# A hybrid Fourier, attention and mixture-of-experts network on one Trainium2 core: the depthwise convolution as plain float32 matmuls, the routing tables in groups of eight, splits queued behind a flag, and pools that release tile by tile

## The chip, the cores and the metric

The kernel runs on one core of one Trainium2 chip. The core has a matrix engine (TensorE, PE in the profile, with its weight loads as PEld), a vector engine (VectorE, DVE), a scalar engine (ScalarE, ACT), GpSimd (POOL) and SyncE (SP), which here only issues DMA transfers. Each engine works through its own queue in order. The metric is the device time of one execution in microseconds; less is better.

## What is computed

Two layers over 2048 tokens of 1024 channels, with a small context. Layer 0 mixes tokens by a Fourier transform of half of its channels and a windowed attention of the rest; layer 1 is a convolution module; behind each stands a mixture of 16 experts, of which each token takes two. All of it is float32.

```python
def _conformer_conv(h, pw1_w, pw1_b, dw_w, dw_b, ln_g, ln_b, pw2_w, pw2_b):
    a, g = jnp.split(h @ pw1_w + pw1_b, 2, axis=-1)
    u = a * jax.nn.sigmoid(g)
    u = lax.conv_general_dilated(u, dw_w[:, None, :], ...,      # 31 taps, each channel by itself
                                 feature_group_count=u.shape[-1]) + dw_b
    u = jax.nn.silu(_layernorm(u, ln_g, ln_b))
    return u @ pw2_w + pw2_b

def _grouped_moe(h, router_w, router_b, w_gate, w_up, w_down):
    scores = jax.nn.sigmoid(t @ router_w)
    ...                                   # best group of 4 by its top two, then the top 2 experts in it
    order = jnp.argsort(flat_e)           # the assignments sorted by expert,
    padded = (counts + 127) // 128 * 128  # each expert's in blocks of 128 slots
    ...
    def expert_block(args):
        tok, e = args
        xb = t_pad[tok]
        return (silu(xb @ w_gate[e]) * (xb @ w_up[e])) @ w_down[e]
```

## The kernel before

**Products.** Nearly every product of two float32 matrices is made of three matmuls of a shorter float type (written fp32r): a number is split into a high part `h` (a cast, by ScalarE) and a low part `l` (the number less its high part, by VectorE, in some places GpSimd), and `mm3` (lines 76 to 82) adds hh, hl and lh. `split` (line 70) issues the cast and the subtraction.

**Stages.** In order: attention (0 to some 640 us), the Fourier part (fold, transform, output; to 900), the routing of the first experts (900 to some 1005), 41 blocks of the first experts (to 1880), the convolution's first matrix pw1 (to 2282), the depthwise convolution (to 2496), pw2 with layer norm (to 2800), the second routing and the second experts.

**The convolution** (`_conv`, lines 1497 to 1552). The 1024 channels are 64 groups of 16, and a tile has 16 channels by 8 phases of the tokens on its 128 partitions and 256 positions along them (token = 8 x position + phase). A group's convolution is five matmuls with banded 128x128 weights, each for the same data shifted by one position; the bands `th`, `tl` are the tap table `wth`, `wtl` times a mask `mk` that keeps each channel to itself. The loop runs over 32 steps of two groups: fetch `u` from memory (SP), split it twice, once for each of two shifts (`uh`, `ul`: ScalarE and VectorE), for each group make `th` (VectorE) and `tl` (GpSimd), run five times `mm3` (15 matmuls of 256 columns), add the bias while emptying PSUM (ScalarE, line 1539) and store `v` (ScalarE's queue). In the first eight steps the weights of pw2 are loaded and split too, and behind every fourth step SP loads `v` back for what follows.

**The routing** (`tail_start`, `choose`, `route`, `moe`). For each tile of 128 tokens the router's logits are made (`lgs`, `lgp`), the experts ranked on VectorE (`E`, one-hot rows), and counted by matmuls (`pr`). For the last two tiles, 14 and 15, the normalised row is made by `last()` at the end of the tail, by a copy on ScalarE and two operations on GpSimd (line 914). Then `route` builds a table of 6144 slots (`tab`, 32 matmuls over `vt`, line 1122): `vt` holds for each slot column n and tile t whether the token of this row belongs there, laid out [n, t], and each matmul picks one t out of every 16 elements. `slot_i` is the list of tokens by slot; `gather` (GpSimd, an indirect DMA, line 1187) fetches the tokens of a block into `xg`, and `xtr` transposes and splits them. The weights of the first block come as six tiles `raw` and are split by `wsplit` into `wh` (ScalarE) and `wl` (four operations for a tile): tile 0 on GpSimd behind the last normalisation, the other five on VectorE behind `placed`, the making of `slot_i`.

**The order** comes from a scheduler that places instructions in program order by engine, with `issue_after` holding an instruction back behind another. Buffers come from pools (`tile_pool`). A pool that opens where an older one closed takes its memory, and in this version its first users wait for all that was under way on the old pool as a whole, whichever tile they touch.

**The fold** (`_fold`, line 674) opens such pools behind the attention: `pe<-z` clears eight PSUM banks, then for each of eight channel groups VectorE builds sums and differences of `h` (`p`, `eo`, `d`, `de`, lines 697 to 707), which PE multiplies by tables (`wqh`, `wql`). The first `h` is in memory on chip already, the others are loaded by SP (line 694), and GpSimd's queue loads the tables `ch`, `cl`, `sh`, `sl`.

## Time and profile before

| | us |
|---|---|
| median of three runs | 3701.32 (3699.11 to 3705.8) |
| the profiled execution | 3704.51, its span 3702.6 |
| PE busy | 3225.4 (87%) |
| VectorE busy | 2490.0 (67%) |
| ScalarE busy | 1520.0 (41%) |
| GpSimd busy | 1003.4 (27%) |
| mean granted clock of TensorE | 0.928 |

Busy time is the time in which an engine had an instruction running. [...] The 1.9 us between span and time lie around the program. A row's number in brackets is the idle time of its engine just before it, and what ended it.

### The profile page before, as it was taken

Reading aid. Unit: us, or ns where it says so; the run is one execution under the profiler, and the core shown is the slowest. Engines: PE = TensorE matmul, PEld = TensorE weight load, DVE = VectorE, ACT = ScalarE, POOL = GpSimd, SP = SyncE. Lnnn points to the kernel's source line nnn. Section 1 sums busy time; section 2 is a strip of 40 time slices with the busy share of each in tenths; the row PEclk is TensorE's granted clock in tenths of the full one; section 3 lists DMA queues with packets and bytes.
Section 4 is the critical chain, followed back from the end, with each engine's and each line's share of the span. In section 5 each row is a group of like instructions: output and inputs, shape, how many; then the busy total and the mean of one; then the engine's idle time right before and its main releaser. Section 6 shows DMA issues by size and latency. Waiting matters only on the chain. (4 is left out here: it accounts for less than half of the span.)

```text
span 3702.6 us, 57945 instructions
## 1 busy us (share of the span) xinstructions
PE 3225.4 (87%) x20868; PEld 2863.5 (77%) x20868; DVE 2490.0 (67%) x5261; ACT 1520.0 (41%) x3353; POOL 1003.4 (27%) x774
## 2 busy tenths in 40 slices
PE   7899998688599899989979998776877999999997
PEld 4677776576488888888879998665666888889897
DVE  5889988758766554656463323988997687784554
ACT  4666767233344222444342222333333465561331
POOL 2343433533311111111130001554542222212221
PEclk9999999799789999999989999887987999999999
DMA  6322222454575655656532213322325676773452
GB/s 231 93 86 79 93 71 96 148 167 179 205 248 193 204 176 165 218 183 201 180 103 46 46 35 85 117 90 96 108 97 207 226 294 252 285 296 116 169 180 105
DMA packets 258094, 571.07 MB, mean 154 GB/s; under 512 B 94809, under 2 KB 142945, under 8 KB 230113
## 3 DMA queue, kind: packets, MB, share of 16 engines
q1 hardware_dynamic: 178704, 386.75, 30.0%
q0 software_dynamic: 42512, 138.39, 12.7%
q10 hardware_dynamic: 36416, 40.09, 3.2%
q8 instruction: 253, 4.15, 0.4%
q14 instruction: 209, 1.70, 0.1%
HBM read 436.12 MB, written 133.73 MB: 154 GB/s over the span
## 5 line engine op out<-in xcount | busy, mean ns | idle before, releaser
L1181 ACT CAST wh<-raw 128x512 fp32r<-128x512 f32 x768 | 455.3, 621 | 153.7 <-DVE y L1287 70.1
L1184 DVE TENSOR_TENSOR wl<-raw,wh 128x512 fp32r<-128x512 f32 x760 | 484.2, 684 | 23.5 <-ACT wh L1181 19.5
L79 PE MATMUL gps<-wh,xt0h 128*128 128x256 f32 x1344 | 403.5, 300 | 64.2 <-issue 22.8
L81 PE MATMUL gps<-wh,xt0l 128*128 128x256 f32 x1344 | 396.8, 295 | 16.0 <-DVE wl L1184 11.1
L80 PE MATMUL gps<-wl,xt0h 128*128 128x256 f32 x1344 | 395.7, 294 | 0.0
L79 PE MATMUL gps<-wh,xt1h 128*128 128x256 f32 x1280 | 368.2, 288 | 18.6 <-issue 18.6
L81 PE MATMUL gps<-wh,xt1l 128*128 128x256 f32 x1280 | 364.0, 284 | 6.5 <-DVE wl L1184 5.9
L80 PE MATMUL gps<-wl,xt1h 128*128 128x256 f32 x1280 | 363.9, 284 | 0.0
L79 PEld LDWEIGHTS gps<-wh,xt0h 128*128 128x128 f32 x1344 | 273.5, 204 | 75.6 <-issue 61.9
L1219 ACT ACTIVATE sg<-gps 128x256 f32<-128x256 f32 x164 | 63.3, 386 | 588.2 <-PE gps L81 558.0
L79 PE MATMUL ag<-hh,p1h 128*128 128x256 f32 x1024 | 292.0, 285 | 3.6 <-DVE u L1481 2.1
L1221 DVE TENSOR_TENSOR hid<-sg,gps 128x256 f32<-128x256 f32 x164 | 68.6, 418 | 333.4 <-PE gps L81 333.4
L80 PE MATMUL ag<-hl,p1h 128*128 128x256 f32 x1024 | 290.8, 284 | 0.0
L81 PE MATMUL ag<-hh,p1l 128*128 128x256 f32 x1024 | 290.6, 284 | 0.0
L1187 POOL DMA_INDIRECT xg<-f_d,slot_i x88 | 98.0, 1113 | 705.0 <-PE xps L1194 676.5
L81 PEld LDWEIGHTS gps<-wh,xt0l 128*128 128x128 f32 x1344 | 273.4, 203 | 18.5 <-DVE wl L1184 12.8
L79 PE MATMUL yps<-wh,hh 128*128 128x512 f32 x656 | 280.0, 427 | 0.0
L80 PEld LDWEIGHTS gps<-wl,xt0h 128*128 128x128 f32 x1344 | 274.1, 204 | 0.6
L79 PEld LDWEIGHTS gps<-wh,xt1h 128*128 128x128 f32 x1280 | 246.6, 193 | 22.4 <-issue 20.9
L81 PE MATMUL yps<-wh,hl 128*128 128x512 f32 x656 | 259.0, 395 | 0.0
L80 PE MATMUL yps<-wl,hh 128*128 128x512 f32 x656 | 258.4, 394 | 0.0
L81 PEld LDWEIGHTS gps<-wh,xt1l 128*128 128x128 f32 x1280 | 246.6, 193 | 6.6 <-DVE wl L1184 6.5
(846 smaller groups left out, 9099.2 us busy)
## 6 DMA issues: line engine op xcount, KB each, us to landing
raw<-in_wall SPq DMA_DIRECT2D x202, 1024.0 KB, 8.6
oh<-in_ada_w SPq DMA_DIRECT2D x24, 1024.0 KB, 8.9
racw<-in_ada_w SPq DMA_DIRECT2D x64, 256.0 KB, 2.7
x_d<-x SPq DMA_DIRECT2D x32, 512.0 KB, 6.2
f_d<-f ACTq DMA_DIRECT2D x28, 512.0 KB, 3.2
adaw<-in_ada_w SPq DMA_DIRECT2D x32, 256.0 KB, 5.5
x<-in_x SPq DMA_DIRECT2D x16, 512.0 KB, 4.2
ht_d<-hf ACTq DMA_DIRECT2D x16, 512.0 KB
```

The costliest lines, as they stand in the source:

```text
L79: mm(ps, ah, bh, start=first, stop=False)
L80: mm(ps, ah, bl, start=False, stop=False)
L81: mm(ps, al, bh, start=False, stop=last)
L1181: nc.scalar.copy(h, r)
L1184: (nc.gpsimd if pool else nc.vector).tensor_tensor(l, r, f32(h), ALU.subtract)
L1187: return self.nc.gpsimd.indirect_dma_start(self.xg[s % 2], None, self.f[self.lay], bass.IndirectOffsetOnAxis(self.slot_i[:, s:s + 1], 0))
L1219: one = nc.scalar.activation(sg, g, AF.Silu)
L1221: return one, nc.vector.tensor_tensor(hid[:, b * 256:b * 256 + 256], sg, u, ALU.mult)
```

## The change

Five things at once.

1. **The convolution** takes plain float32 matmuls on `u` itself: five for a group in place of 15, no splits of `u` or of the taps. `u` lies in six buffers with zero borders, so that a shift is an offset, and is fetched five steps ahead. `th` and the PSUM tile have four buffers each, the staging tile of pw2's weights two.
2. **Eights.** The slot table's columns are laid out [m, t, j] with n = 8m + j: each matmul reads eight adjacent elements, and the vectors that are compared and multiplied along t are made in eight copies first (`slb`, `tk8`, `tl8`, `part`).
3. **Flags.** `went` is set by GpSimd behind the second gather, VectorE copies it (`routed2`), and all six tiles' splits, now all on VectorE, are queued behind this copy. Loads of the next weights all go through SP.
4. **The last normalisation** of tiles 14 and 15 is two operations on VectorE, and tile 14's comes earlier in the program.
5. **All pools** are opened with `reuse_waits="tile"`: the first user of a new tile waits only for what used that piece of memory.

```diff
-    def wsplit(self, i, pool=False, after=None):
+    def wsplit(self, i, after=None):
...
-            (nc.gpsimd if pool else nc.vector).tensor_tensor(l, r, f32(h), ALU.subtract)
+            nc.vector.tensor_tensor(l, r, f32(h), ALU.subtract)
...
             def last():
-                with self.tc.issue_after((self.scored if i == 15 else self.copied).ins):
-                    nc.scalar.activation(f, x, AF.Copy, scale=r)
-                for op, z in ((ALU.mult, G2), (ALU.add, S2)):
-                    self.normed = nc.gpsimd.tensor_tensor(f, f, z, op)
+                nc.vector.scalar_tensor_tensor(f, x, r, G2, ALU.mult, ALU.mult)
+                nc.vector.tensor_tensor(f, f, S2, ALU.add)
...
-                eq = ys[0][:, h * i:h * i + h].bitcast(BF16).rearrange("p (n t) -> p n t", n=NS)
+                eq = ys[0][:, h * i:h * i + h].bitcast(BF16).rearrange("p (m x) -> p m x", m=M)
...
-                nc.tensor.matmul(tab, self.oh[:, i, k], vt[:, :, :, k], start=False, stop=i + k == T)
+                nc.tensor.matmul(tab, self.oh[:, i, k], vt[:, :, :, 8 * k:8 * k + 8], start=False, stop=i + k == T)
...
+                with tc.issue_after(g.ins):
+                    nc.gpsimd.memset(self.went, 1.0)
+                with tc.issue_after(self.placed.ins):
+                    went = nc.vector.tensor_copy(self.routed2, self.went)
                 for i in range(6):
-                    if i < (1,1)[lay]:
-                        with tc.issue_after(self.scored.ins), tc.issue_after(self.normed.ins):
-                            self.wsplit(i, True)
-                        with tc.issue_after(g.ins):
-                            self.load(i, 17 * lay + 1, nc.gpsimd)
-                    else:
-                        with tc.issue_after(g.ins), tc.issue_after(self.placed.ins):
-                            self.wsplit(i)
-                        self.load(i, 17 * lay + 1)
+                    with tc.issue_after(self.scored.ins), tc.issue_after(went.ins):
+                        self.wsplit(i)
+                    self.load(i, 17 * lay + 1)
...
-        UO = [[[wp.tile([P, 2, 260], F32R, name=f"u{x}{sh}{i}") for x in "hl"] for sh in range(2)] for i in range(2)]
+        U = [(up if i < 3 else wp).tile([P, 2, 260], F32, name=f"u{i}") for i in range(6)]
...
+        for b in range(5):
+            fetch(b)
         for b in range(32):
-            if b % 4 == 1 and b < 28:
-                taps(2 * b + 6)
-            u = up.tile([P, 2, 256], F32, name="u", tag="u", bufs=3)
-            nc.sync.dma_start(u, u4[:, 2 * b:2 * b + 2, :])
-            uo = UO[b % 2]
-            for sh in range(2):
-                uh, ul = uo[sh]
-                self.split(uh[:, :, 2 - sh:258 - sh], ul[:, :, 2 - sh:258 - sh], u)
+            if b < 27:
+                fetch(b + 5)
+            u = U[b % 6]
...
-                th = tp.tile([P, 5, 16, 8], F32R, name="th", tag="th")
-                tl = tp.tile([P, 5, 16, 8], F32R, name="tl", tag="tl")
-                nc.vector.tensor_tensor(th, f32(wth[:, g])[:, :, None, :].to_broadcast([P, 5, 16, 8]), mks, ALU.mult)
-                nc.gpsimd.tensor_tensor(tl, f32(wtl[:, g])[:, :, None, :].to_broadcast([P, 5, 16, 8]), mks, ALU.mult)
-                ps = pp.tile([P, 256], F32, name="cv", tag="cv")
+                th = tp.tile([P, 5, 16, 8], F32, name="th", tag="th", bufs=4)
+                nc.vector.tensor_tensor(th, wt[:, g][:, :, None, :].to_broadcast([P, 5, 16, 8]), mks, ALU.mult)
+                ps = pp.tile([P, 256], F32, name="cv", tag="cv", bufs=4)
                 for j in range(5):
-                    uh, ul = uo[j % 2]
-                    s = slice(j - j % 2, j - j % 2 + 256)
-                    a = [x[:, j].rearrange("p c q -> p (c q)") for x in (th, tl)]
-                    self.mm3(ps, a[0], a[1], uh[:, i, s], ul[:, i, s], j == 0, j == 4)
+                    nc.tensor.matmul(ps, th[:, j].rearrange("p c q -> p (c q)"), u[:, i, j:j + 256], start=j == 0, stop=j == 4)
...
-            with tc.tile_pool(name="fc", bufs=1) as cp, tc.tile_pool(name="fp", bufs=1, space=PSUM) as pp:
+            with tc.tile_pool(name="fc", bufs=1, reuse_waits="tile") as cp, tc.tile_pool(name="fp", bufs=1, space=PSUM, reuse_waits="tile") as pp:
```

VectorE's queue at the start of the convolution (`u<-ag` is the end of pw1, `ul`, `wtl` and `p2l` are low halves), before:

```order
L1481 SCALAR_TENSOR_TENSOR u<-ag,p1b,sg 128x32x8 x11
L1565 MEMSET on 128x128
L74 TENSOR_TENSOR wtl<-wt,wth 128x320
L1531 TENSOR_TENSOR th<-wth,mk 128x640
L74 TENSOR_TENSOR ul_34360<-u,uh_34359 128x2x256
L74 TENSOR_TENSOR ul_34362<-u,uh_34361 128x2x256
L1531 TENSOR_TENSOR th<-wth,mk 128x640
L74 TENSOR_TENSOR wtl<-wt,wth 128x320
```

and after:

```order
L1487 SCALAR_TENSOR_TENSOR u<-ag,p1b,sg 128x32x8 x11
L1529 TENSOR_TENSOR th<-wt,mk 128x640 x4
L1559 MEMSET on 128x128
L1529 TENSOR_TENSOR th<-wt,mk 128x640
L74 TENSOR_TENSOR p2l<-raw_34401,p2h 128x1024
L1529 TENSOR_TENSOR th<-wt,mk 128x640
```

Four bands now stand right behind pw1's last `u`, with no split between them.

VectorE's queue where the slots of the first experts are known (`routed` is the flag, `wl` a weight split, `xt0l` the first block's tokens), before:

```order
L1125 TENSOR_REDUCE slot_i<-tab 128x48
...
L1137 TENSOR_SCALAR ch<-ch 128x1
L1184 TENSOR_TENSOR wl_10073<-raw_10083,wh_10072 128x512 x4
L1184 TENSOR_TENSOR wl_10067<-raw_10084,wh_10066 128x512 x3
L74 TENSOR_TENSOR xt0l<-xps,xt0h 128x512 x2
L1184 TENSOR_TENSOR wl_10067<-raw_10084,wh_10066 128x512
L1184 TENSOR_TENSOR wl_10069<-raw_10085,wh_10068 128x512 x4
L1184 TENSOR_TENSOR wl_10075<-raw_10086,wh_10074 128x512 x4
```

and after:

```order
L1132 TENSOR_REDUCE slot_i<-tab 128x48
...
L1144 TENSOR_SCALAR ch<-ch 128x1
L1346 COPY routed<-routed 128x1
L1191 TENSOR_TENSOR wl_10069<-raw_10080,wh_10068 128x512 x3
L74 TENSOR_TENSOR xt0l<-xps,xt0h 128x512 x2
L1191 TENSOR_TENSOR wl_10069<-raw_10080,wh_10068 128x512
L1191 TENSOR_TENSOR wl_10071<-raw_10081,wh_10070 128x512 x4
L1191 TENSOR_TENSOR wl_10065<-raw_10082,wh_10064 128x512 x4
```

The copy of the flag stands ahead of the first split, three splits instead of seven stand ahead of the tokens, and 21 instead of 13 behind them before the next other work.

VectorE's queue at the logits of tile 15 (`ch<-lgs` are the logits, the operations behind them rank the experts), before:

```order
L103 TENSOR_SCALAR roots<-tny 128x1
L946 SCALAR_TENSOR_TENSOR ch<-lgs,roots,shift 128x16
L1017 TENSOR_TENSOR ch<-ch,rb 128x32
L1009 TENSOR_TENSOR ch<-ch 128x128
L1011 TENSOR_TENSOR ch<-ch,rc 128x128
```

and after:

```order
L946 SCALAR_TENSOR_TENSOR ch<-lgs,roots,shift 128x16
L911 SCALAR_TENSOR_TENSOR f<-x,roots,G_8583 128x1024
L1016 TENSOR_TENSOR ch<-ch,rb 128x32
L912 TENSOR_TENSOR f<-f,S_8588 128x1024
L1008 TENSOR_TENSOR ch<-ch 128x128
```

The two operations of the last normalisation now stand among the ranking's.

## Rows read from the trace of the kernel before

**Rows 1.** Windows: stretch, its length, each engine's busy time (instructions), granted clock, DMA.

```profile
960.00:1060.00 100.00, 68.34 (x475) 62.36 (x476) 59.70 (x136) 25.31 (x47) 27.95 (x17) 0.71 0.51 169
...
1900.00:2290.00 390.00, 380.65 (x3172) 379.98 (x3170) 132.02 (x313) 98.04 (x205) 20.19 (x30) 0.99 0.24 52
2290.00:2500.00 210.00, 152.08 (x961) 144.50 (x961) 183.83 (x162) 70.75 (x138) 121.86 (x63) 0.83 0.38 114
```

**Rows 2.** The tiles `th` and `cv`: durations (min/median/max ns), then PE's idle time (us, times) until.

```profile
L1531 DVE TENSOR_TENSOR th<-wth,mk x64: 808/825/2191, 2287.1 to 2489.2; 128x640 fp32r<-128x640 f32 x64
...
  DVE th L1531: 50.0, 19
```

**Rows 3.** Timeline, one step of the convolution: start, us, what, [idle before <- releaser].

```profile
2415.86 2.88 DVE L1531 TENSOR_TENSOR th<-wth,mk 128x640 fp32r<-128x640 f32 x2
...
2418.15 0.36 PE L79 MATMUL cv<-uh,th 128*128 128x256 f32 x1 [2.84 <-DVE th L1531]
```

**Rows 4.** Timeline, from pw1 into the convolution, and its last matmul.

```profile
2281.89 0.28 PE L81 MATMUL ag<-hh,p1l 128*128 128x256 f32 x1
...
2282.71 0.65 DVE L1481 SCALAR_TENSOR_TENSOR u<-ag,p1b,sg 128x256 f32<-128x256 f32 x1 [5.06 <-ACT sg L1479]
...
2286.23 0.46 ACT L73 CAST wth<-wt 128x320 fp32r<-128x320 f32 x1 [3.56 <-DMA u_d<-u]
...
2288.16 0.55 PE L79 MATMUL cv<-uh,th 128*128 128x256 f32 x1 [5.99 <-ACT wth L73]
...
2495.58 0.28 PE L81 MATMUL cv<-uh,tl 128*128 128x256 f32 x1
```

**Rows 5.** Float32 matmuls of other stages: tile views (ns), then timelines.

```profile
L1587 PE MATMUL mean<-sq,on x12: 378/379/382, 2550.2 to 2741.2; 128*128 128x256 f32 x12
...
L196 PE MATMUL ada<-adaw,cc x64: 592/592/1057, 6.0 to 38.1; 128*2 128x512 f32 x64
...
2549.94 0.40 PE L81 MATMUL wo<-p2h,zl 128*128 128x512 f32 x1
...
2550.17 0.59 PE L1587 MATMUL mean<-sq,on 128*128 128x256 f32 x2
...
2550.84 0.40 PE L80 MATMUL wo<-p2l,zh 128*128 128x512 f32 x1
...
2551.07 0.40 PE L81 MATMUL wo<-p2h,zl 128*128 128x512 f32 x1
...
2809.13 1.94 PE L944 MATMUL lgs<-rw,f 128*128 128x16 f32 x16
```

**Rows 6.** Timeline, the start of the Fourier fold.

```profile
679.20 1.23 DVE L697 TENSOR_TENSOR p<-h 128x1023 f32<-128x1023 f32 x1 [11.18 <-DMA x_d<-x]
...
683.94 0.56 PE L79 MATMUL pe<-wqh,eh 128*128 128x260 f32 x1 [13.73 <-ACT eh L73]
...
686.80 2.90 DVE L697 TENSOR_TENSOR p<-h 128x1023 f32<-128x1023 f32 x1 [2.77 <-DMA h<-ht_d]
```

**Rows 7.** Timeline, routing of the first experts.

```profile
964.19 2.40 DVE L96 SCALAR_TENSOR_TENSOR tna<-tny,tnv 128x1 f32<-128x1 f32 x1
...
969.51 0.22 DVE L96 SCALAR_TENSOR_TENSOR tna<-tny,tnv 128x1 f32<-128x1 f32 x1
...
980.38 0.20 PE L1034 MATMUL pr<-E,trb 128*128 128x48 bf16 x1 [14.12 <-DVE E L1027]
...
986.48 5.77 PE L1122 MATMUL tab<-xg,oh 128*128 128x96 bf16 x32 [4.34 <-DVE xg L1120]
...
993.12 4.29 DVE L1184 TENSOR_TENSOR wl<-raw,wh 128x512 fp32r<-128x512 f32 x7
...
993.38 4.94 POOL L1187 DMA_INDIRECT xg<-f_d,slot_i  x1 [11.88 <-DVE ch L1137]
```

**Rows 8.** Timeline, routing of the second experts.

```profile
2828.31 0.20 PE L1034 MATMUL pr<-E,trb 128*128 128x48 bf16 x1 [11.88 <-DVE E L1027]
...
2842.95 1.00 POOL L1187 DMA_INDIRECT xg<-f_d,slot_i  x1 [11.06 <-DVE ch L1135]
```

More of the change, by code (lines that the diff above doesn't have):

```diff
@@ L140, in route_consts @@
         nc, io = self.nc, self.io
-        cm = self.tc.tile_pool(name="rt", bufs=1, side="right")
+        cm = self.tc.tile_pool(name="rt", bufs=1, side="right", reuse_waits="tile")
         pool = cm.__enter__()
@@ L167, in route_consts @@
         self.tl = pool.tile([P, 2, NT], BF16, name="tl")
-        self.routed = pool.tile([P, 1], F32, name="routed")
+        flags = pool.tile([P, 3], F32, name="routed")
+        self.routed, self.went, self.routed2 = [flags[:, i:i + 1] for i in range(3)]
         self.E = {T: pool.tile([P, 16 * T + 16], BF16, name=f"E{T}") for T in (4, 2)}
@@ L568, in _attention @@
         self.hp.__exit__(None, None, None)
-        self.hp = self.tc.tile_pool(name="h0", bufs=1, side="right")
+        self.hp = self.tc.tile_pool(name="h0", bufs=1, side="right", reuse_waits="tile")
         self.h0 = self.hp.__enter__().tile([P, L], F32, name="h0")
@@ L641, in fourier @@
                 for nms in ("emo", "p"):
-                    yps.append(tc.tile_pool(name="fy" + nms, bufs=1, side="right"))
+                    yps.append(tc.tile_pool(name="fy" + nms, bufs=1, side="right", reuse_waits="tile"))
                     y = yps[-1].__enter__()
@@ L660, in raw_open @@
     def raw_open(self, lay, a=0, b=6):
-        cm = self.tc.tile_pool(name=f"raw{lay}{a}", bufs=1, side="right")
+        cm = self.tc.tile_pool(name=f"raw{lay}{a}", bufs=1, side="right", reuse_waits="tile")
         rp = cm.__enter__()
@@ L1445, in weights @@
                     for name, side in (("c1b", "left"), ("c1r", "right")):
-                        more.append(self.tc.tile_pool(name=name, bufs=1, side=side))
+                        more.append(self.tc.tile_pool(name=name, bufs=1, side=side, reuse_waits="tile"))
                         more.append(more[-1].__enter__())
@@ L1488, in conv_start @@
         nc, io = self.nc, self.io
-        self.cvp = self.tc.tile_pool(name="cv0", bufs=1, side="right")
+        self.cvp = self.tc.tile_pool(name="cv0", bufs=1, side="right", reuse_waits="tile")
         p = self.cvp.__enter__()
@@ L1499, in _conv @@
         up, wt, mk, db = self.cv
-        wth = wp.tile([P, 64, 5, 8], F32R, name="wth")
-        wtl = wp.tile([P, 64, 5, 8], F32R, name="wtl")
-        def taps(g):
-            s = slice(g, g + 8)
-            self.split(wth[:, s], wtl[:, s], wt[:, s])
-        taps(0)
         wh, wl = self.pw2
```

87 lines of the change are left out of this document (47 added, 40 removed).

## The prediction

> **What bounds the kernel now.** I read the table of windows first, with the stages as its stretches, to see where TensorE (PE) does not fill its time, because the dense stages are already full. The stage before the convolution keeps PE busy for 380.65 of 390 us at a clock of 0.99; the convolution has 152.08 of 210 us at 0.83; and the 100 us in which the first mixture of experts is routed have 68.34 at 0.71 [rows 1]. Those are the two kinds of place that the change rewrites.
>
> Then I read the convolution by its tile, for what PE waits for. It sits idle 50.0 us, in 19 pieces, until VectorE (DVE) has made a band of taps `th` [rows 2]. One such piece shows why: two bands take 2.88 us on DVE where an undisturbed one takes 0.825 (the median), and PE starts 2.84 us late [rows 2, 3]. DVE also makes the low halves of `u` and shares the time with GpSimd, which makes `tl`. So the convolution is fed by DVE, not held by its matmuls: pw1 runs 3172 matmuls of the same 256 columns in 380.65 us, 0.12 us each [rows 1], so the 960 of the convolution would take 115 us if fed, and the stage takes 213.7 (from the last matmul of pw1, 2281.89 + 0.28, to the last of the convolution, 2495.58 + 0.28) [rows 4].
>
> Last I read the timelines at the joints of the stages: the start of the Fourier fold, where PE is idle 13.73 us [rows 6], and the two routings, where it is idle 14.12 and 11.88 us in one piece and more behind it [rows 7, 8].
>
> **Convolution, the main term.** Removed: 640 of 960 matmuls, all work of ScalarE on `u` (two casts a step), two DVE subtractions a step, every `tl` on GpSimd, the taps' split. Added: 320 matmuls in plain float32. What one costs is the number on which this forecast rests. The trace has such a matmul, `mean<-sq,on`, 256 columns: each call shows as two records of 379 ns, side by side as "x2" in the timeline [rows 5]. Around one pair the timeline goes from 2549.94 to 2550.84 with one wo matmul, the pair and another wo matmul; wo matmuls start 0.23 apart (2550.84 to 2551.07), so the pair costs 0.90 - 2 x 0.23 = 0.44 us, 0.22 a record [rows 5]. A second way gives nearly the same: a 512-column float32 record lasts 592 ns and a 256-column one 379, so 256 columns cost 0.213 us [rows 5]. Loading 128x128 float32 weights for every record doesn't add to it: 16 float32 matmul records, each with another set of weights and 16 columns, take 1.94 us, 0.12 each [rows 5], less than 0.22. So PE needs 320 x 0.44 = 140.8 us, against 115 for the three-term product: by PE alone the change is a loss, and it gains only by what feeds it.
>
> [...]
>
> What feeds it now: per step of two groups PE needs 4.40 us. DVE has two `th` of 0.825, 1.65 us; even at the 2.88 that a disturbed pair took it would keep up [rows 2, 3]. In the first eight steps a split of 1024 elements comes on top, some 1.3 us by the 640 of a band. ScalarE keeps two evictions. GpSimd is idle, so DVE is undisturbed. `u` comes five steps (22 us) ahead in six buffers. The start: the last `u` of pw1 is written at 2282.71 + 0.65; DVE then makes the first band, 0.82, so PE starts near 2284.3 where it started at 2288.16 [rows 4], because the cast ahead of it, 3.56 us behind the store of `u` [rows 4], is gone, and the tile-wise pools carry no such wait over to `th`. From 2282.2: 2.1 + 140.8 = 143, and 1.7 for slow records behind the pause, 144.7 against 213.7. **Term: -69 us.** [...] What follows the convolution (the last store, its load, the variance, then pw2) keeps its chain, and moves with it.
>
> **The fold's start.** PE waits 13.73 us until 683.94. The chain behind it: DVE's `p<-h` starts at 679.20 after 11.18 us for the landing of the store `x_d` [rows 6]; that store has nothing to do with `h`, it is a wait that the whole pool carried. With waits by tile, `p` could start near 668 and PE 11 us sooner. But its second half, `h` of the next channel group, lands at 686.8 today (DVE waits 2.77 for it) [rows 6], and if it is asked for earlier it shares the queues with 4 MB of tables; half of the gain then comes back as a wait. Term -6, ends 0 and -11. The other joints have no such wait on their chain: 0.
>
> **Routing of the first experts.** Before, GpSimd's normalisation of the last two tiles and its four weight splits run beside DVE's small operations, and seven of these take 1 to 2.4 us (one of them takes 2.40 at 964.19 and 0.22 at its next turn, undisturbed) [rows 7]; together some 11 us, all on the chain to `E`. The change takes that work off GpSimd and puts four operations of 1024 elements on DVE, 1.23 each by the one of 1023 [rows 6]: -11 + 5 = -6, of which I take 5.5, at `E` (which PE gets at 980.38 before). The table of slots, 32 matmuls in 5.77 us [rows 7], reads its table eight adjacent elements at a time where it picked every sixteenth: nearest is the 0.12 of a 256-column matmul for its 96 columns in place of 0.18, -2 (ends 0 and -3). So the slots are known about 7.5 us sooner. Then the flag: all 24 splits wait on DVE until both gathers are issued. The first gather takes 4.94 us beside DVE's splits [rows 7], where the one of the second layer takes 1.00 without them [rows 8], so the flag lets it go in about 1 us and costs DVE 2 us of waiting. The four splits that GpSimd made now stand on DVE too, 4 x 0.61 (seven take 4.29 [rows 7]) = 2.5. And the tokens, for which DVE waits in the midst of its splits, are there earlier; of the gather's 3.9 I count half, -2. The load of tile 0's next weights moves from GpSimd's queue to SP's, behind the stores that the gathers need, so it holds neither up: 0. Net: -7.5 + 2 + 2.5 - 2 = -5, ends +3 (the stretched operations were hidden) and -10.
>
> **Routing of the second experts.** The same, 11.88 us until `E` at 2828.31 [rows 8]; there the first gather is quick already, 1.00 [rows 8], so the flag only delays the splits (+2) and four more of them are DVE's (+2.5); at the slots I take the same -7.5 and one more for splits on GpSimd that stretch operations behind `E` there: -8.5 + 4.5 = -4; ends +4 and -9.
>
> **Sum.** -69 - 6 - 5 - 4 = -84. The profiled execution took 3704.5 (span 3702.6 and 1.9 around it), 3.2 above the median of the three runs; against the median 3701.3 - 84 = 3617.
>
> **The rivals.**
> *Float32 matmuls run at the low clock in the convolution (slower).* The place is the 640 records in a row. [...] It turns to a loss from 0.33 us a record. For it: the convolution's clock is 0.83 today, and each time PE was starved it came back slowly. Against: in the trace 592 ns (the high clock) is both the lowest and the median of 64 float32 records, though PE there also waits for data [rows 5], and pw1, as dense, has 0.99 [rows 1]. 5%.
> *The splits behind the flag cost more than the routing gains.* If the stretched operations overlapped other waits and DVE sets the first slot, both routings lose 5: 3701.3 - 69 - 6 + 10 = 3636. For it: the splits, not the gathers, are what DVE does last before the first slot. Against: `E` ends both of the long idle stretches [rows 7, 8]. 13%.
> *SyncE's queue starves the convolution.* On SP the loads of `v` stand between fetches of `u`, each behind the landing of a store of the same step; if each of some eight such places held the queue past the lead by a step of PE, 4.4 us, 35 us come back: 3652. Against: the lead is 22 us, and each of these stores is due before the buffer for the next fetch is free. 8%.
> *The change doesn't do what it says at the joints:* if waits by tile bring nothing, 3623, inside the forecast.
>
> **How the numbers follow.** Forecast, 3601 to 3632 (the ends of the small terms and of the pair's price, not all at once): 70%. More than that, under 3601: 4%. Splits, 3632 to 3645: 13%. SP, 3645 to 3690: 8%. Low clock, above 3701: 5%. The range 3601 to 3648 leaves out 4% below and some 12% above. About 0.2% is what a measurement of this kernel can tell from no change: faster by more 94%, within 1%, slower 5%.
>
> **What would show it.** In the trace after: 640 records `cv<-u,th` about 0.22 apart with no idle time of PE on `th`, the stage near 145 us at a clock near 1; first `pe` matmul of the fold 0 to 11 us after the end of `pe<-z`, then a longer wait for `h`; DVE's small operations at 0.15 to 0.3 before `E`; the first gather at 1 us. Wrong if PE in the convolution waits for `u` or `th`, if records are 0.4 apart, or if PE's idle time before the first slot grows by what the splits take.

## The result and the profile after

The changed kernel takes 3582.01 us in the median of four runs (3578.59 to 3586.66), beside 3703.56 for the kernel before (3699.11 to 3710.68): a ratio of 0.967, 95% interval 0.965 to 0.969, or 121.5 us less. The prediction said 3617 with a range of 3601 to 3648. The direction and the main term held; the gain is 37 us larger than forecast and lies outside the range.

The totals of the page after: TensorE is now busy for a larger share of a shorter span, with less work on every engine.

```profile
span 3584.9 us, 56780 instructions
...
PE 3192.6 (89%) x20548; PEld 2825.3 (79%) x20548; DVE 2356.2 (66%) x5207; ACT 1478.8 (41%) x3281; POOL 840.2 (23%) x690
```

**The convolution** first, by its window (length, busy time of PE, PEld, DVE, ACT, POOL, granted clock, DMA share, GB/s) and its tiles (durations min/median/max in ns, then PE's idle time in us and times). It answers to [rows 1, 2]:

```profile
2245.00:2388.00 143.00, 140.00 (x650) 121.95 (x649) 68.58 (x94) 38.17 (x74) 0.20 (x4) 1.00 0.54 169
...
L1532 PE MATMUL cv<-u,th x640: 377/379/483, 2247.9 to 2387.0; 128*128 128x256 f32 x160
...
  DVE th L1529: 0.5, 1
...
L1529 DVE TENSOR_TENSOR th<-wt,mk x64: 808/824/827, 2247.0 to 2378.8; 128x640 f32<-128x640 f32 x64
```

The granted clock is 1.00 of full speed where it was 0.83, PE waits 0.5 us for a band of taps where it waited 50.0, and no `th` takes longer than 0.827 us where some took 2.19. The 640 records from 2247.9 to 2387.0 are (2387.0 - 2247.9) / 639 = 0.218 us apart, 0.435 a matmul. Its entry, by the timeline, answers to [rows 4]:

```profile
2245.67 0.28 PE L81 MATMUL ag<-hh,p1l 128*128 128x256 f32 x1
...
2246.49 0.65 DVE L1487 SCALAR_TENSOR_TENSOR u<-ag,p1b,sg 128x256 f32<-128x256 f32 x1 [5.06 <-ACT sg L1485]
2246.99 3.01 DVE L1529 TENSOR_TENSOR th<-wt,mk 128x640 f32<-128x640 f32 x4
2247.90 3.48 PE L1532 MATMUL cv<-u,th 128*128 128x256 f32 x15 [1.95 <-issue]
```

PE is idle for 1.95 us where it was for 5.99. From the last matmul of pw1 to the last of the convolution, start to start, it is 141.3 us where it was 213.7.

**The fold** (timeline; VectorE's first `p`, PE's first `pe`, and the `p` of the second group), answering to [rows 6]:

```profile
667.68 1.34 DVE L698 TENSOR_TENSOR p<-h 128x1023 f32<-128x1023 f32 x1
...
674.54 0.59 PE L79 MATMUL pe<-wqh,eh 128*128 128x260 f32 x1 [4.63 <-ACT eh L73]
...
680.12 1.23 DVE L698 TENSOR_TENSOR p<-h 128x1023 f32<-128x1023 f32 x1 [6.38 <-DMA h<-ht_d]
```

`p` starts 11.5 us sooner, with no wait for the store `x_d`; PE starts 9.4 us sooner and waits 4.63 us for 13.73. The second `h` is waited for longer, 6.38 us for 2.77, as foreseen, but `p` still runs 6.7 us sooner, and the fold's last `pe` matmul comes 8.8 us sooner (753.51 for 762.31).

**A joint behind it**, from the transform to the output of the Fourier part, which the prediction did not price. PE's first `wo` matmul there, before (timeline):

```profile
803.40 0.77 PE L79 MATMUL wo<-ch,Ye0h 128*128 128x512 f32 x1 [3.22 <-issue]
```

and after, with no idle time:

```profile
791.22 0.40 PE L79 MATMUL wo<-ch,Ye0h 128*128 128x512 f32 x1
```

**The first routing** (timeline), answering to [rows 7]; the first row is the last `wo` matmul of the Fourier part, `xps` are the transposes of a block's tokens, `hps` those of its hidden rows:

```profile
951.86 0.39 PE L81 MATMUL wo<-wqh,Yp3l 128*128 128x512 f32 x1
...
959.56 0.15 DVE L100 SCALAR_TENSOR_TENSOR tny<-tna,tny 128x1 f32<-128x1 f32 x1
...
966.64 0.20 PE L1033 MATMUL pr<-E,trb 128*128 128x48 bf16 x1 [6.75 <-DVE E L1026]
...
972.04 2.97 PE L1129 MATMUL tab<-xg,oh 128*128 128x96 bf16 x32 [4.99 <-DVE xg L1127]
...
976.14 1.05 POOL L1194 DMA_INDIRECT xg<-f_d,slot_i  x1 [32.62 <-DVE ch L1144]
...
980.50 1.97 PE L1201 MATMUL xps<-ident,xg 128*128 128x128 f32 x8 [3.84 <-DMA xg<-f_d,slot_i]
983.74 12.72 DVE L1191 TENSOR_TENSOR wl<-raw,wh 128x512 fp32r<-128x512 f32 x21
996.38 0.22 DVE L1064 TENSOR_TENSOR ch<-ch,o 128x64 f32<-128x64 f32 x1
...
999.57 0.41 DVE L1228 TENSOR_TENSOR hid<-sg,gps 128x256 f32<-128x256 f32 x1
1000.04 0.69 PE L1233 MATMUL hps<-ident,hid 128*128 128x128 f32 x2 [7.74 <-DVE hid L1228]
...
1005.40 0.97 PE L1169 MATMUL tw<-ys,oh 128*128 128x48 bf16 x32
```

PE waits 6.75 us for `E` where it waited 14.12; the slot table takes 2.97 us for 5.77, the gather 1.05 for 4.94. On the other side, 21 splits in one piece of 12.72 us stand ahead of `hid`, the first block's hidden rows, then 3.2 us of small operations that begin the slot weights, and PE waits 7.74 us for `hid`. The last row has no answer in the rows shown of before: `tw`, the table of slot weights, which is built like `tab`. In the kernel before each of its three groups of 32 matmuls looks like the second row here; the first is the last `wo` matmul again (timeline of before):

```profile
959.12 0.39 PE L81 MATMUL wo<-wqh,Yp3l 128*128 128x512 f32 x1
...
1021.36 3.03 PE L1162 MATMUL tw<-ys,oh 128*128 128x48 bf16 x32
```

Where the 117 us of span went, stage by stage, worked out from the starts of PE's matmuls in the two timelines (predicted terms beside them; a block has two pairs of `hps` matmuls, one for each half of its hidden rows; block k, from 0 to 40, runs from its first pair to the next block's):

| stage | before | after | difference | predicted |
|---|---|---|---|---|
| to the fold's first matmul | 683.9 | 674.5 | -9.4 | -6 |
| to `E` of the first routing | 296.4 | 292.1 | -4.3 | -5.5 |
| `E` to the first `hps` | 36.3 | 33.4 | -2.9 | +0.5 |
| block 0 from its first pair to its second, which holds the `tw` groups | 16.7 | 10.2 | -6.5 | 0 |
| from there to the first pair of block 40 | 827.6 | 814.5 | -13.1 | 0 |
| last pw1 matmul to last of the convolution | 213.7 | 141.3 | -72.4 | -69 |
| last of the convolution to `E` of the second routing (with pw2) | 332.7 | 325.6 | -7.1 | -5.5 |
| `E` to the first `hps`, second experts | 32.7 | 33.7 | +0.9 | +1.5 |
| block 0 from its first pair to its second, second experts | 15.0 | 9.3 | -5.7 | 0 |
| from there to the first pair of the last block | 798.7 | 802.2 | +3.5 | 0 |

(Differences are rounded by themselves. The second routing's -4 is divided as its working has it: -5.5 ahead of `E`; behind it -2 for the table, -1 for the stretched operations and 4.5 for the flag and the splits.)

Each column is one trace. In a second trace of the changed kernel (`after2` below) the way to the first `E` is 5.0 us shorter, pw2 to the second `E` 5.6 shorter and the blocks of the second experts 6.2 longer, so a few us in these rows are not clear of the scatter. A nearer measure for the work ahead of `E` is the way from the last `wo` matmul to `E`: 21.3 us before, 14.8 after, and the same in `after2`; for the second routing 19.5 before, 15.1 and 14.5 after.

### The profile page after: what moved, and what is told of

It reads as the page before. It is cut to its first block, busy times and chain, and to the rows that moved or that the text cites. A ratio compares the mean times of both kernels' runs of the same rounds, so it can differ in the third digit from the quotient of the medians.

```text
span 3584.9 us, 56780 instructions
## 1 busy us (share of the span) xinstructions
PE 3192.6 (89%) x20548; PEld 2825.3 (79%) x20548; DVE 2356.2 (66%) x5207; ACT 1478.8 (41%) x3281; POOL 840.2 (23%) x690
## 5 line engine op out<-in xcount | busy, mean ns | idle before, releaser
L81 PE MATMUL gps<-wh,xt0l 128*128 128x256 f32 x1344 | 395.3, 294 | 24.7 <-DVE wl L1191 18.4
L79 PE MATMUL ag<-hh,p1h 128*128 128x256 f32 x1024 | 292.1, 285 | 3.6 <-DVE u L1487 2.1
L1194 POOL DMA_INDIRECT xg<-f_d,slot_i x88 | 89.4, 1016 | 735.7 <-PE xps L1201 655.1
L79 PEld LDWEIGHTS gps<-wh,xt1h 128*128 128x128 f32 x1280 | 246.8, 193 | 17.7 <-issue 13.1
```

Source lines behind the costliest of these rows:

```text
L79: mm(ps, ah, bh, start=first, stop=False)
L81: mm(ps, al, bh, start=False, stop=last)
L1194: return self.nc.gpsimd.indirect_dma_start(self.xg[s % 2], None, self.f[self.lay], bass.IndirectOffsetOnAxis(self.slot_i[:, s:s + 1], 0))
```

## The experiments

The kernels came to several chips; the kernel before takes 3695.6 to 3713.8 us on them. So each is given by its ratio to the kernel before on the same chip; the changed kernel's is 0.967 and, on another chip, 0.969.

### The parts one by one: the convolution alone, the pools alone

`conv_only` is the kernel before with the new `_conv` alone; `tile_only` the kernel before with the pools' option alone:

```diff
-        with tc.tile_pool(name="mw2", bufs=1) as wp2, ...
+        with tc.tile_pool(name="mw2", bufs=1, reuse_waits="tile") as wp2, ...
```

> The kernel before with the changed convolution alone. Theory A (the convolution's gain is its own: PE-bound float32 matmuls in place of a stage fed by VectorE): the stage from the last matmul of pw1 to the last of the convolution goes from 213.7 us to 141 to 146, the whole 68 to 73 us faster, near 3633. Theory B (part of the gain needs the tile-wise pools): the start of the convolution still waits for the store of u, and the stage takes 150 us or more.

> The kernel before with tile-wise waits in all pools and nothing else. Theory A (they are worth at the joints what the undo run lost there, and in the experts' stages too): 25 to 35 us faster, near 3673, with the first experts' stage (hid of block 0 to the first matmul of pw1) near 850 us where before has 880. Theory B (only the joints): 9 to 13 us faster, near 3692.

Measured: `conv_only` 3644.39 against 3713.78, 0.982 [0.979, 0.985], -66 us by the ratio. Its convolution has the same pace of matmuls as the changed kernel's; the stage takes 144.9 us for 141.3, because its first matmul still comes 5.2 us behind pw1's last, not 2.2. `tile_only` 3674.99 against 3713.78, 0.991 [0.989, 0.994], -32 us. The prediction gave the pools -6. In the trace of `tile_only` the fold's start brings 9.8 us of it, the way to `E` 5, the convolution's entry 3.5, the blocks of the first experts some 9, and 5 come at the first gathers (timeline):

```profile
977.78 1.03 POOL L1187 DMA_INDIRECT xg<-f_d,slot_i  x1 [11.23 <-DVE ch L1135]
...
978.08 4.29 DVE L1184 TENSOR_TENSOR wl<-raw,wh 128x512 fp32r<-128x512 f32 x7
979.12 4.11 POOL L1187 DMA_INDIRECT xg<-f_d,slot_i  x1 [0.30 <-PE pt L1143]
```

There the first gather is issued 0.3 us ahead of the splits and takes 1.03 us; the second runs beside seven splits and takes 4.11. So the slow gather of [rows 7] is slow beside the splits, and gets out of their way with the pools' waits alone, without a flag. It seems to wait the splits out: a slow gather ends 0.9 us behind the last of the seven splits here, in [rows 7] and in `undo_flags` below. Why a gather is slow beside the splits, 4.11 us for 1.03, these rows do not show.

### The pools undone

`undo_tile` is the changed kernel with the option off everywhere, `undo_tile_moe` with it off in the experts' pools alone (`mw2`, `mw0`, `mw1`, `mx`, `mt`, `mp`, `raw`).

> The changed kernel with all pools' waits as before. Theory A (the pool-wide wait at the fold was worth all that the trace shows, and the start of the convolution a little): the first product of the fold waits 13 to 14 us again, 9 us slower there, and the first matmul of the convolution some 2 to 3 us later: 9 to 13 us slower, 3591 to 3595. Theory B (as the prediction had it, half of the fold's gain comes back): 5 to 7 us slower. Theory C (tile-wise waits also help at the switches from one expert's weights to the next): 20 us slower or more, with the difference growing through the first experts' stage.

> The changed kernel with pool-wide waits in the pools of the experts' stages alone. Theory A (the waits of these pools hold the experts' loop): the first experts' stage is 15 us longer, 3597. Theory B (the longer stage of the undo run is no wait of these pools but comes with another placing of the program or another time at which the stage begins): within 5 us of 3582.

Measured: `undo_tile` 3622.03 against 3707.41, 0.977 [0.976, 0.978]; `undo_tile_moe` 3601.23 against 3713.78, 0.970 [0.967, 0.973]. Undone, the pools cost 31 to 36 us by the ratios, as `tile_only` gains 32. The fold and the convolution's entry in `undo_tile` (timeline):

```profile
680.79 1.22 DVE L698 TENSOR_TENSOR p<-h 128x1023 f32<-128x1023 f32 x1 [10.15 <-DMA x_d<-x]
...
685.53 0.56 PE L79 MATMUL pe<-wqh,eh 128*128 128x260 f32 x1 [12.70 <-ACT eh L73]
...
2274.38 3.03 DVE L1529 TENSOR_TENSOR th<-wt,mk 128x640 f32<-128x640 f32 x4 [2.67 <-DMA u_d<-u]
```

The wait for `x_d` is back at the fold, 11 us for PE against the changed kernel; and the first bands wait for the store `u_d`, so PE starts 3 us later there. The joint into the Fourier output goes with the pools' waits in every trace: PE is idle there for 2.2 to 3.7 us in the five kernels in which the pools there wait as a whole (3.10 in `undo_tile`), and not at all in the thirteen others. The blocks of the first experts (second pair of block 0 to first pair of block 40) take 831.8 us in `undo_tile` and 825.4 in `undo_tile_moe`, where the changed kernel takes 814.5 and 812.7 in its two traces. Whether the pools' waits are the reason for that is taken up below.

### Eights undone

```diff
-                nc.tensor.matmul(tab, self.oh[:, i, k], vt[:, :, :, 8 * k:8 * k + 8], start=False, stop=i + k == T)
+                nc.tensor.matmul(tab, self.oh[:, i, k], vt[:, :, :, k], start=False, stop=i + k == T)
```

(and the vectors and `tw` with it: the `route` of before).

> The changed kernel with the slot tables laid out as before, so that each matmul for tab and tw picks every sixteenth element. Theory A (the matmuls of the tables, tw above all, lie on PE's path and cost by how their operand is laid out): tab goes back from some 3 us to 5.8 and the three tw from 1.0 to 3.0 us each, in both layers, so (2.8 + 6.1) x 2 = 18 us slower than the changed kernel, near 3600. Theory B (as the prediction had it, only tab matters, 2 us a layer): 4 us slower, near 3586.

Measured: 3603.93 against 3707.41, 0.973 [0.971, 0.975], 14 to 20 us over the changed kernel by the ratios. The timeline of `undo_eights`:

```profile
964.45 5.77 PE L1121 MATMUL tab<-xg,oh 128*128 128x96 bf16 x32 [4.68 <-DVE xg L1119]
...
1000.67 3.08 PE L1161 MATMUL tw<-ys,oh 128*128 128x48 bf16 x32
```

Both prices are those of before. The slot table is 5.77 - 2.97 = 2.8 us a layer; the three groups of `tw` are 3 x 2.05 = 6.2 us a layer in block 0, on PE, which does nothing else meanwhile. For both layers that is 18 us, of which the prediction had 4.

### The last normalisation and the flag undone

`undo_last` gives `last()` back to ScalarE and GpSimd; `undo_flags` takes the wait for both gathers away and gives tile 0's splits back to GpSimd:

```diff
-                with tc.issue_after(self.placed.ins):
-                    went = nc.vector.tensor_copy(self.routed2, self.went)
...
-                    with tc.issue_after(self.scored.ins), tc.issue_after(went.ins):
-                        self.wsplit(i)
+                    if i < (1,1)[lay]:
+                        with tc.issue_after(self.scored.ins), tc.issue_after(self.normed.ins):
+                            self.wsplit(i, True)
```

> The changed kernel with the normalisation of tiles 14 and 15 on ScalarE and GpSimd as before. Theory A (GpSimd beside VectorE stretches the small operations that E waits for): 5 us a layer, 8 to 11 us slower, 3590 to 3593, with single-column operations of 2 us in the trace again. Theory B (the stretched operations were hidden): within 2 us of 3582.

> The changed kernel with the weight splits as before: tile 0 on GpSimd, the others on VectorE without the flag, next load of tile 0 on GpSimd's queue. Theory A (the flag buys the first gather of layer 0 its 4 us, and costs VectorE four splits per layer): the first gather of layer 0 takes near 5 us again, the first tokens come 4 us later there, but the first hid does not: within 4 us of the changed kernel, 3578 to 3586. Theory B (the flag is where the unexplained 20 us of the first experts' stage come from): 15 to 20 us slower, near 3600.

Measured: `undo_last` 3596.12 against 3707.41, 0.969 [0.967, 0.971]; `undo_flags` 3587.63, 0.968 [0.966, 0.969]. By the changed kernel's two ratios the last normalisation is worth 1 to 7 us, which the times alone do not tell from nothing, and the flag nothing. The traces tell more: from the last `wo` matmul to `E` it takes 19.7 us in `undo_last` and 17.7 in `undo_flags`, where the changed kernel takes 14.8; in the second routing 18.4 and 16.9 for 15.1 and 14.5. So the last normalisation is worth some 5 us ahead of the first `E` and 3 to 4 ahead of the second. In `undo_last` a small operation beside GpSimd's last tile takes 2.29 us, and ends with GpSimd's, where it takes 0.15 after (timeline):

```profile
958.85 2.35 POOL L915 TENSOR_TENSOR f<-f,G 128x1024 f32<-128x1024 f32 x1 [14.63 <-ACT f L913]
...
958.93 2.29 DVE L100 SCALAR_TENSOR_TENSOR tny<-tna,tny 128x1 f32<-128x1 f32 x1
...
971.39 0.20 PE L1035 MATMUL pr<-E,trb 128*128 128x48 bf16 x1 [10.45 <-DVE E L1028]
```

and in `undo_flags` the first gather is slow again, though the time is not (timeline):

```profile
970.87 0.20 PE L1033 MATMUL pr<-E,trb 128*128 128x48 bf16 x1 [11.87 <-DVE E L1026]
...
980.12 4.30 DVE L1191 TENSOR_TENSOR wl<-raw,wh 128x512 fp32r<-128x512 f32 x7
980.38 4.96 POOL L1194 DMA_INDIRECT xg<-f_d,slot_i  x1 [10.48 <-DVE ch L1144]
...
988.79 1.97 PE L1201 MATMUL xps<-ident,xg 128*128 128x128 f32 x8 [7.89 <-DMA xg<-f_d,slot_i]
```

From `E` to the first `xps` matmul it takes 17.9 us where the changed kernel takes 13.9; from there to the first `hps` 14.7 where the changed kernel takes 19.5. What the flag gains at the gather it loses behind it: three splits in place of seven stand ahead of the tokens, but 21 in place of 13 behind them, ahead of `hid`. In the second routing, where the gather was quick already, it only loses: from `E` to the first `hps` 33.7 us with it and 28.9 without. Taking tile 0's splits off GpSimd gives 2 to 3 us ahead of each `E`, and the sum is nothing. That points to a better version.

### A version that keeps the flag and lets `hid` through

The splits of tiles 4 and 5 are the weights that the first block needs last. `w45` puts them later in the program; `w45b` also makes them, and the making of the slot weights (`weights`), wait for the hidden rows:

```diff
-                for i in range(6):
-                    with tc.issue_after(self.scored.ins), tc.issue_after(went.ins):
-                        self.wsplit(i)
-                    self.load(i, 17 * lay + 1)
+                def put(a, b):
+                    for i in range(a, b):
+                        ...
+                put(0, 4)
...
+        if s == 0:
+            with self.tc.issue_after(b.ins):
+                self.put(4, 5)
+        c, d = half(1, th)
+        if s == 0:
+            with self.tc.issue_after(d.ins):
+                self.put(5, 6)
...
-            self.weights()
+            with self.tc.issue_after(b.ins):
+                self.weights()
```

> The changed kernel with the splits of the first block's last two weight tiles (needed only by its second product) moved behind the first half of the hidden layer on VectorE. Theory A (the 24 splits set the first hid, for which PE waits 7.7 us in the trace after): first hid 5 us sooner in both layers, 3 to 10 us faster, near 3575. Theory B (the second product waits for them instead): within 2 us of 3582.

> The changed kernel with the splits of the first block's last two weight tiles, and the slot weights, ordered behind the first hid on VectorE (in the run w45 the scheduler had put the moved splits ahead of it again). Theory A (the splits set the first hid): the first hid comes 6 to 9 us sooner after the first tokens in both layers, and the whole is 5 to 15 us faster than the changed kernel beside it. Theory B (the second product then waits for the same splits): within 3 us.

> The changed kernel again, as the measure for the three runs beside it: 0.967 of before, and a first experts' stage within 3 us of the 860 us of its first trace if that stage repeats from run to run.

`w45` took 3586.32 against 3713.78, 0.967 [0.965, 0.970]: the scheduler had put the eight splits ahead of `hid` again, so it says nothing of the order. `w45b` took 3564.84 (3556.19 to 3574.8); `after2`, the changed kernel once more on the same chip, 3580.1 (3576.05 to 3585.86), and the kernel before 3695.59: ratios 0.965 [0.962, 0.968] and 0.969 [0.966, 0.971]. `w45b` is 15 us under the changed kernel, with no run of one among those of the other, and the fastest of all. Its timeline:

```profile
975.45 1.97 PE L1201 MATMUL xps<-ident,xg 128*128 128x128 f32 x8 [3.79 <-DMA xg<-f_d,slot_i]
978.68 7.91 DVE L1191 TENSOR_TENSOR wl<-raw,wh 128x512 fp32r<-128x512 f32 x13
986.50 0.42 DVE L1228 TENSOR_TENSOR hid<-sg,gps 128x256 f32<-128x256 f32 x1
987.23 0.38 PE L1233 MATMUL hps<-ident,hid 128*128 128x128 f32 x2
```

Thirteen splits stand ahead of `hid` in place of 21, and no slot weights; PE has it 11.8 us after the tokens, not 19.5; in the second routing 12.4. From `E` to the first `hps` that is 7.8 and 7.2 us, which is the gain: of the 8.0 us by which `hid` itself comes sooner behind the tokens than in the trace of `after`, the eight splits give 4.8 (12.72 less 7.91) and the slot weights 3.2.

### The experts' blocks: a wait, or something else

The blocks of the first experts got 13 us shorter, though the change leaves their code alone but for the pools' waits. (The loop of 840 and 824 us in the expectations is taken over a stretch some 10 us longer than the table's; its differences compare.) `pad4`, `pad8`, `pad16` and `pad24` are the changed kernel with 4 to 24 tiny matmuls more at the fold, far ahead; `bpad8` and `bpad24` the same on the kernel before:

```diff
             nc.tensor.matmul(ps[l], z[:, :P], z, start=True, stop=False)
+        for l in range(8):
+            nc.tensor.matmul(ps[l % 8][:, :2], z[:, :P], z[:, :2], start=False, stop=False)
```

> The changed kernel with 8 extra matmuls of two columns behind the clearing of the fold's PSUM banks (they add zeros; under 1 us of work). Theory A (the experts' stages cost by where their code lies: a taken branch of TensorE whose target must be fetched takes 3 to 7 us, and which ones do is shifted by the instructions ahead): the pattern of TensorE's long branches changes and with it the first experts' stage (block 0 to pw1), by 5 us or more either way. Theory B (placing of code does not matter, the pool-wide waits themselves do): within 3 us of the changed kernel run beside it.

> The same with 24 extra matmuls of two columns (under 2 us of work). Theory A: again another pattern of long branches, and a first experts' stage that differs by 5 us or more from the changed kernel or from the 8-matmul version. Theory B: within 4 us of the changed kernel run beside it.

> The changed kernel with four such matmuls. Place of the code: the loop lies between the 818 and 836 us seen so far, apart from the 823 to 825 of the changed kernel by some us in either direction, and the time moves as far. If the pads' loss of 14 us came from their work or from a wait at the fold, four cost half of eight, 7 us, and the loop stays at 824.

> The changed kernel with sixteen such matmuls. Place of the code: loop between 818 and 843. If it is the pads' work or a wait at the fold: 14 us over the changed kernel, as 8 and 24 were, with the loop at 834 to 836.

> The kernel before with eight matmuls of two columns more at the start of the fold (under 2 us of work), else unchanged. If the loop of the first experts takes its time from the place of its code, it moves by 5 us or more from the 840 us that it takes in the kernel before (a gain as well as a loss is open), and the time with it, outside 3695 to 3705 in terms of a kernel before of 3700. If the changed kernel's shorter loop comes from its waits, the loop stays at 838 to 843 and the time within 0 to +3 us.

> As bpad8, with 24 such matmuls. Place of the code: the loop is at another value than 840, and need not be that of bpad8. Waits: the loop stays at 838 to 843 and the time within 0 to +5 us.

Measured: `pad8` 3594.08 and `pad24` 3595.05, beside 3580.1 for `after2` on the same chip: 14 us for less than 2 us of work. On another chip `pad4` 0.970 [0.968, 0.972], `pad16` 0.969 [0.968, 0.971], 5 to 11 and 2 to 7 us over the changed kernel by its two ratios; `bpad8` 1.000 [0.999, 1.001], `bpad24` 0.999 [0.998, 1.000], -5 us. The blocks in the traces (us, from a block's first `hps` pair to the next block's; some blocks of many), and of the 56 branches of TensorE's weight queue at the loop's line those over 2 us, which are explained below:

| | before | bpad8 | bpad24 | after | after2 | pad4 | pad8 | pad16 | pad24 |
|---|---|---|---|---|---|---|---|---|---|
| block 5 | 26.5 | 28.2 | 25.7 | 23.7 | 23.7 | 23.9 | 25.5 | 26.3 | 27.5 |
| block 7 | 18.3 | 18.3 | 18.3 | 18.3 | 18.3 | 18.3 | 18.3 | 18.3 | 18.3 |
| block 8 | 29.4 | 27.8 | 21.7 | 24.6 | 24.5 | 28.5 | 29.0 | 27.6 | 27.1 |
| block 19 | 26.6 | 24.9 | 21.3 | 30.1 | 29.7 | 26.5 | 26.6 | 25.2 | 24.5 |
| second pair of block 0 to first of block 40 | 827.6 | 830.4 | 817.9 | 814.5 | 812.7 | 823.0 | 823.3 | 828.4 | 825.1 |
| branches over 2 us | 19 | 19 | 15 | 16 | 16 | 17 | 17 | 18 | 19 |

Some blocks (7 is one, nearly every second) are alike to 0.1 us in every kernel; the others differ, and up to block 24 the two traces of the changed kernel agree to 0.5 us in each (behind it single blocks differ by up to 2.5, the sum by 1.8). So most of the difference belongs to the program, not to the execution. PE runs the same 5270 matmuls over this stretch in before, `bpad24`, `after2` and `pad8`, and is busy for 763.0 to 763.6 us in the last three and 768.2 in before; the rest of the difference is idle time. This is the window of before and that of `bpad24`:

```profile
1033.40:1861.10 827.70, 768.22 (x5270) 704.72 (x5269) 464.11 (x785) 313.20 (x597) 124.22 (x104) 0.96 0.62 197
```

```profile
1028.20:1846.10 817.90, 763.44 (x5270) 700.79 (x5269) 464.17 (x785) 313.20 (x597) 125.58 (x104) 0.97 0.63 199
```

In the blocks that differ PE's weight queue takes branches. Block 8 in four kernels, by the line of the loop (ns min/median/max of the two branches), and the idle time of PE at the same matmul of the block. Before:

```profile
L1369 PEldq COMPARE_BRANCH  x2: 5382/5732/6083, 1202.0 to 1208.6; - x2
...
1214.10 0.55 PE L79 MATMUL gps<-wh,xt1h 128*128 128x256 f32 x1 [7.64 <-issue]
```

`bpad24`, the same kernel with 24 matmuls ahead:

```profile
L1371 PEldq COMPARE_BRANCH  x2: 367/2920/5473, 1197.5 to 1198.4; - x2
...
1204.00 0.36 PE L79 MATMUL gps<-wh,xt1h 128*128 128x256 f32 x1 [2.02 <-DVE wl L1186]
```

`after2`:

```profile
L1375 PEldq COMPARE_BRANCH  x2: 281/3581/6881, 1172.0 to 1172.8; - x2
...
1179.84 0.36 PE L79 MATMUL gps<-wh,xt1h 128*128 128x256 f32 x1 [3.33 <-DVE y L1294]
```

`pad8`, the same with eight matmuls ahead:

```profile
L1377 PEldq COMPARE_BRANCH  x2: 5002/5522/6043, 1172.8 to 1179.3; - x2
...
1184.44 0.55 PE L79 MATMUL gps<-wh,xt1h 128*128 128x256 f32 x1 [7.22 <-issue]
```

Where both branches take 5 to 6 us, PE is idle for more than 7 us and goes on with a matmul of 0.55 us, not 0.36; where one takes 0.3 to 0.4, it is idle for 2 to 3.3. In all four this matmul starts 0.16 to 0.17 us behind the end of the second branch. A few matmuls far ahead turn the one into the other, in both kernels and in both directions. Over the loop of `after2` the 56 branches of this line go from 65 to 6881 ns, with a median of 311.

The traces also show what a long branch waits for. One queue, `q8`, carries instructions in packets of 16384 bytes. Its row of the page of `after` (packets, MB, share), then its rows for the first long branch of block 8 in before (1202.0 to 1208.1 us) and for the long one in `after2` (1172.8 to 1179.7); for the short one in `after2` (1172.05 to 1172.33) there is no such row:

```profile
q8 instruction: 249, 4.08, 0.5%
...
q8 instruction: 1, 0.02, 1.1%
...
q8 instruction: 2, 0.03, 2.5%
```

Over this stretch of the eighteen traces (before, after and sixteen runs) all 308 branches of this line that take over 2 us overlap such a packet, and of the 700 shorter ones one does, of 2.0 us. A long branch ends 1.3 to 2.1 us behind the last packet that ends in it. Every kernel moves 83 or 84 of these packets there; what differs is how many of them a branch has to wait for, 15 to 19.

What follows, and what does not. It is shown that the blocks gain or lose 10 us without any change of waits: four to 24 matmuls more give the changed kernel 823.0 to 828.4 us for 812.7 and 814.5, and the kernel before with 24 more has 817.9 for 827.6. (`bpad24`'s trace is of its fastest execution, 3688.43 of a median of 3703.78, so its 817.9 is its good end.) The length goes with the number of long branches, whatever the waits: kernels with 15 or 16 of them take 812.7 to 818.8 us, those with 17 to 19 take 823.0 to 831.8, `undo_tile` (19, 831.8), `undo_tile_moe` (17, 825.4) and `tile_only` (16, 818.8) among them; only `w45b` stands apart (17, 813.1). `bpad8`, of which a move was expected, kept its 19 and its length. So the changed kernel's 13 us come with three long branches fewer, 16 for 19. Open is whether waits by tile give a part: at equal counts the kernels that have them are the shorter ones (17: 823.0 and 823.3 for 825.4; 19: 825.1 for 827.6 to 831.8), but these are few traces. Nor is it shown which instructions' places decide that a branch has to wait, or that the long ones are the taken ones.

## Why the prediction was wrong, point by point

Three steps failed: the joints and blocks that the pools' new waits were said to leave alone, put at 0; the second table of the eights, which had no term; and the half of the fold's gain that was to come back.

**What bounds the kernel, and the convolution's term: right.** PE waited for VectorE's `th`; with one `th` a group and nothing of GpSimd beside it, it waits no more, and PE's own matmuls set the stage. The price of a float32 matmul was taken as 0.44 us from one pair in the timeline [rows 5]; measured 0.435, and the stage at 141.3 us for 144.7. The 1.7 us put in for slow records behind the pause did not come: the window has a clock of 1.00. From the first to the last of the 640 records it is 139.1 us.

**The fold: the mechanism right, half of it wrongly given back.** The wait for `x_d` went as said, 11.5 us at `p`. The longer wait for the second `h` came too, 6.38 us, but the step "half of the gain then comes back" failed: that `p` still ran 6.7 us sooner than before, and at the fold's last matmul 8.8 of the 9.4 us were left (in `after2` 6.9 of 6.9). -9.4 for -6.

**The pools elsewhere: the step that failed most by part.** "The other joints have no such wait on their chain: 0." The pools alone are worth 32 us, not 6. One such joint is the start of the Fourier output, where PE waited 3.22 us and then does not. At the convolution's entry their share was in the convolution's term. At the first gather the rows showed how little was missing, though not that a pool's wait was it [rows 7]: `wl` starts at 993.12 and the gather at 993.38; in `tile_only` the gather starts 0.3 us ahead and is quick. The blocks of the experts, put at 0 too, lost 13 us (9 in `tile_only`), which go with three long branches of TensorE fewer; what of it is the waits' stays open.

**The eights: a term that was left out.** The prediction priced `tab` (-2; measured -2.8) and did not look for a second table of the same layout. `tw` has three groups of 32 such matmuls in each layer, 6.2 us, all on PE's path: -12 us for both layers, the largest miss that one edit undone shows by itself.

**The small operations ahead of `E`: right.** They do go from 2.3 to 0.15 us, PE's longest wait for `E` fell from 14.12 to 6.75, and the way from the last `wo` matmul to `E` from 21.3 to 14.8: -6.5 us for the -5.5, and -4.4 to -5.0 in the second routing. The stage from the fold to `E` shows only -4.3 (-9.3 in `after2`), because the Fourier output ahead of it took 160.6 us (157.7) for 155.7; the cause of that stays open.

**The flag: right in sum, by other numbers.** With the four splits and the gather it was priced at +2.5 in the first routing and +4.5 in the second. Measured from `E` to the first `hps`, against `undo_flags`: 4 us sooner at the tokens and 5 later at `hid` in the first, +0.8 in sum, and +4.8 in the second. With the 2 to 3 us that each `E` comes sooner it is nothing in the time.

**The rivals.** *The low clock in the convolution* did not come: 1.00, records of 379 ns. *SyncE's queue* did not starve it: PE's idle time in the convolution names `issue` at its start and `th`, 0.5 us, and never `u`. *The splits behind the flag* is the rival whose mechanism was true: they do set the first `hid`, 5 us later, with the slot weights behind them. It was wrong only in what it left to the other parts, and `w45b` shows it: take eight splits and the slot weights out of the way and 15 us come.

**The range** failed because the terms that were put at zero had no ends. The blocks of the experts had none, though two kernels with the same blocks can differ there by 10 us; `tw` had none because it was not seen. The forecast also counts an upper end of the pair's price; that was the author's estimate and no run shows it: the 640 records gave 0.435 us a matmul for the 0.44.

## What to carry to other kernels

When a change alters the layout of a table, list every instruction that reads such a table, on the other side of the stage too, before pricing one of them. A reorder that clears a slow gather or a slow small operation is worth only what is then late next (here, counted from `E` of the first routing, the flag brought the tokens 4 us sooner and PE's first `hps` 0.8 us later): read what stands between the freed step and the next thing that the busiest engine waits for, and move that as well. And before a gain of 10 us in a loop is put down to an edit, run the unchanged kernel with a few idle instructions ahead of the loop, and count the long branches in both traces.

## What was not expected of the hardware

- Eight matmuls of two columns, far ahead of a loop, changed the time by 14 us on one chip; PE's branches there take 0.07 to 6.9 us in `after2`. Every one over 2 us, in all traces, overlaps a 16384-byte instruction transfer, and how many do changes with the program.
- A matmul that picks every sixteenth element of a bf16 row takes about twice to three times as long as one that reads eight adjacent ones: 5.77 / 32 = 0.18 us for 0.09 with 96 columns, 3.03 / 32 = 0.095 for 0.03 with 48.
- Issuing the same gather takes GpSimd 1.03 to 1.05 us ahead of the splits and 4.11 to 4.96 beside them; a start 0.3 us ahead of them or 0.26 behind decides which.
